# A matmul with a decayed running sum: five of eight scans solved pairwise across ScalarE, GpSimd and VectorE

## The chip, the cores and the metric

The kernel runs on one core of one Trainium2 chip. The metric is the device time of one execution in microseconds, the median of several runs. The kernel before takes 1122.11 us (three runs, 1121.77 to 1122.36).

Each run comes with a state, fast or slow; a run is called slow here when it is over 1.5% above the fastest run of the same kernel.

The engines are named as the profile names them: PE is TensorE, DVE is VectorE, ACT is ScalarE, POOL is GpSimd, SP is SyncE. A trailing q (ACTq, SPq) is the engine's instruction queue, from which it also starts DMA transfers.

## The reference

```
x: (16, 2048, 1024) float32, w: (1024, 1024) float32, decay: (1024,) float32, between 0.05 and 0.95
xw = x @ w
out[:, 0, :] = xw[:, 0, :]
out[:, t, :] = decay * out[:, t - 1, :] + xw[:, t, :]
```

It is a matmul followed by a first-order recurrence along time, separately for each of the 1024 output columns. 134 MB are read and 134 MB are written.

## The kernel before

A "unit" is 1024 time steps of one batch element; there are 32. Each unit has eight "slots" n, one for each block of 128 output columns. TensorE forms the transposed product, with columns on the partitions and time along the free axis, and VectorE's scan instruction runs the recurrence along time (L141, 128x1024, 2252 and 2306 ns). The result is transposed back and stored as 4 MB in four DMAs of 1 MB.

```python
    psp = ctx.enter_context(tc.tile_pool(name="psp", bufs=4, space=bass.MemoryType.PSUM))

    def load(u, l):                       # half a unit: 512 time steps
        xf = xfp.tile([128, 2, NI, CQ], FP32, name="xf")
        for r in range(2):
            for q in range(NQ):
                nc.sync.dma_start(out=xf[q * P:(q + 1) * P, r], in_=...)
        xb = xbp.tile([128, NI, CQ, 2], BF16, name="xb")
        for r in range(2):
            nc.scalar.copy(out=xb[:, :, :, r], in_=xf[:, r])       # the cast, contiguous reads
        xb_of[u, l] = xb
    # turn(u, l): VectorE transposes xb into xt, the operand of the matmul

    for u, (b, h) in enumerate(units):
        for n in range(K):                # 8 slots
            ps = psp.tile([128, TU], FP32, name="ps")
            # ... 16 matmuls into ps ...
            so = sop.tile([128, TU], FP32, name="so")
            nc.vector.tensor_tensor_scan(
                out=so, data0=dec[:, n:n + 1].to_broadcast([128, TU]), data1=ps,
                initial=0.0 if h == 0 else last[n], op0=ALU.mult, op1=ALU.add)
            # ... ScalarE keeps the last column; VectorE transposes the slot before into ot ...
            # ... n == 0: store the unit before; n == 1 and 5: turn and load the next x ...

        def store(u, ot):
            for q in range(NQ):
                nc.scalar.dma_start(out=..., in_=ot[q * P:(q + 1) * P])   # ScalarE's queue
```

The loads are issued from SyncE's queue, the stores from ScalarE's. ScalarE also casts x to bf16, four casts in a unit.

## Time and profile before

| quantity | before | where it is read |
|---|---|---|
| time | 1122.1 us | runs |
| VectorE busy, 400 to 1000 us | 99% | table by stage |
| TensorE busy, same stretch | 91%, granted clock 0.96 | table by stage |
| stores of successive units apart, same stretch | 31.7 us | timeline |
| four stores hold ScalarE's queue, from 312 us on | 9 to 13 us | timeline |

The first part of the page lists busy time, share of the span and number of instructions for each engine:

```profile
PE 932.3 (83%) x4096; PEld 408.4 (36%) x4096; DVE 1013.7 (90%) x584; ACT 324.1 (29%) x257; POOL 0.2 (0%) x4
```

The table by stage shows two stretches from the middle of the run. The columns are the stretch, its length, the busy time and instruction count of each engine, the granted TensorE clock, the share of the DMA engines' time and the GB/s:

```profile
core 0: us, PE busy (x) PEld busy (x) DVE busy (x) ACT busy (x) POOL busy (x), PEclk, DMA share, GB/s
400.00:600.00 200.00, 183.29 (x815) 80.74 (x813) 198.09 (x114) 59.96 (x49) 0.00 (x0) 0.97 1.08 262
...
800.00:1000.00 200.00, 179.59 (x792) 78.78 (x790) 197.74 (x114) 69.02 (x56) 0.00 (x0) 0.95 1.07 267
```

VectorE is busy 198 of every 200 us. TensorE is not far behind with 180 to 183. The groups by line give for each kind of instruction its shapes, its count, then total busy time and the mean in ns of one instruction, and then the engine's idle time just before it with what ended that idle time:

```profile
line engine op names shapes xcount | busy us, mean ns | idle before us <-releasers
L133 PE MATMUL ps<-xt,wsb 128*128 128x512 bf16 x4096 | 932.3, 389 | 157.7 <-DVE xt L106 95.0 <-DVE so L141 42.7 <-DVE wsb L77 19.6
...
L97 ACT CAST xb<-xf 128x2048 bf16<-128x2048 f32 x128 | 310.8, 2474 | 306.2 <-DVE ot L115 100.3 <-DMA xf<-in_x_dram 94.3 <-issue 69.6
L115 DVE STREAM_TRANSPOSE ot<-so 128x1024 f32<-128x1024 f32 x256 | 309.3, 1224 | 3.7
L141 DVE TENSOR_TENSOR_SCAN so<-dec,keep,ps 128x1024 f32<-128x1024 f32 x128 | 295.1, 2306 | 6.4 <-PE ps L133 6.4
L141 DVE TENSOR_TENSOR_SCAN so<-dec,ps 128x1024 f32<-128x1024 f32 x128 | 285.3, 2252 | 20.6 <-PE ps L133 20.6
L106 DVE STREAM_TRANSPOSE xt<-xb 128x2048 f32<-128x2048 f32 x64 | 146.2, 2285 | 44.6 <-ACT xb L97 42.7 <-ACT keep L151 1.8
```

A unit costs VectorE eight scans of 2.28, eight transposes back of 1.22 and two transposes of x of 2.29: together 32.6 us with these means. The scans hardly ever wait for TensorE (6.4 and 20.6 us in all), so VectorE sets the pace.

The busy shares hide something on ScalarE. This is its timeline around one store; the columns are the start, the duration, engine, line, operation and how many instructions are joined:

```profile
start us, us, engine line op out<-in xcount [idle before <-releaser]
498.22 2.48 ACT L97 CAST xb<-xf 128x2048 bf16<-128x2048 f32 x1 [2.10 <-DMA xf<-in_x_dram]
...
503.24 11.40 ACTq L169 DMA_DIRECT2D out_dram<-ot  x4
514.81 4.82 ACT L97 CAST xb<-xf 128x2048 bf16<-128x2048 f32 x2 [14.06 <-DMA out_dram<-ot]
```

The ACTq line is the engine issuing four stores. It takes 11.40 us, and the next cast starts only when it is over. This time is not counted as busy, so ScalarE's 29% says little about how free it is.

The waits of the SyncE queue; the columns are the total, the number of waits and the longest:

```profile
SPq L91 <- DMA out_dram<-ot: 326.5, 36, 30.3
```

Loads wait for stores. In this trace the DMAs issued from SyncE's queue and those from ScalarE's carry the same eight semaphore numbers, 99 to 106. The load that starts at 513.84 waits on number 99, which the store issued at 503.24 carries; the last landing of that store is at 513.82.

### The profile page before, as it was taken

The page shows a single profiled execution, that of the slowest core. Times are in us where ns is not written, and L with a number is a line of the kernel's source. Part 1 is how long each engine was busy: PE and PEld are TensorE (multiplying, and loading weights), DVE is VectorE, ACT ScalarE, POOL GpSimd, SP SyncE. Part 2 cuts the span into 40 slices and gives each one's busy share as a digit, 9 for nine tenths or more (in the row PEclk, how much of TensorE's full clock was granted, in tenths as well). Part 3 has the DMA queues.
Part 4 walks back from the last instruction along what each step waited for, and adds up shares of the span by engine and source line. Part 5 has one row for each costly group of instructions (what it writes and reads, how often), then busy time and mean ns, then how long its engine had stood idle before and what let it go on. Part 6 is the DMA issues. An engine that isn't in the chain of part 4 may idle for free.

```text
span 1123.0 us, 10242 instructions
## 1 busy us (share of the span) xinstructions
PE 932.3 (83%) x4096; PEld 408.4 (36%) x4096; DVE 1013.7 (90%) x584; ACT 324.1 (29%) x257; POOL 0.2 (0%) x4
## 2 busy tenths in 40 slices
PE   0287698796998998989898998989898998989880
PEld 0133243242443443434343443434343443434330
DVE  1295699798999999999999999999999999999991
ACT  2124122242422405151422405151422405151200
POOL 0000000000000000000000000000000000000000
PEclk9997799797999998999999899989999898999995
DMA  9949898999999999999999999999999999999777
GB/s 194 203 81 228 163 268 198 260 275 252 283 272 276 252 276 260 249 273 266 279 264 252 259 279 269 252 274 266 271 264 259 256 277 247 274 278 236 150 145 155
DMA packets 275056, 273.33 MB, mean 243 GB/s; under 512 B 11840, under 2 KB 273984, under 8 KB 275008
## 3 DMA queue, kind: packets, MB, share of 16 engines
q1 hardware_dynamic: 140800, 138.45, 55.5%
q10 hardware_dynamic: 134208, 134.23, 45.5%
q8 instruction: 32, 0.52, 0.2%
q14 instruction: 16, 0.13, 0.0%
HBM read 138.42 MB, written 134.22 MB: 243 GB/s over the span
## 4 chain that ended last, share of the span: by engine, by line
DVE 41%; DMA 27%; issue 9%; SPq 8%; PE 7%; ACTq 3%; ACT 2%; DVEq 0%
DVE so L141 24%; DMA xf<-in_x_dram 15%; DVE ot L115 11%; DMA out_dram<-ot 11%; SPq L91 8%; PE ps L133 7%; DVE xt L106 6%; ACTq L169 3%; ACT xb L97 2%; DMA xf<-in_w_dram 1%; DMA dec<-in_decay_dram 1%; SPq L76 0%; ACT keep L151 0%; ACTq L64 0%; DVE wsb L77 0%
## 5 line engine op out<-in xcount | busy, mean ns | idle before, releaser
L133 PE MATMUL ps<-xt,wsb 128*128 128x512 bf16 x4096 | 932.3, 389 | 157.7 <-DVE xt L106 95.0
L133 PEld LDWEIGHTS <-wsb 128*128 128x128 bf16 x4096 | 408.4, 100 | 681.0 <-issue 204.2
L97 ACT CAST xb<-xf 128x2048 bf16<-128x2048 f32 x128 | 310.8, 2474 | 306.2 <-DVE ot L115 100.3
L115 DVE STREAM_TRANSPOSE ot<-so 128x1024 f32<-128x1024 f32 x256 | 309.3, 1224 | 3.7
L141 DVE TENSOR_TENSOR_SCAN so<-dec,ps 128x1024 f32<-128x1024 f32 x128 | 285.3, 2252 | 20.6 <-PE ps L133 20.6
L141 DVE TENSOR_TENSOR_SCAN so<-dec,keep,ps 128x1024 f32<-128x1024 f32 x128 | 295.1, 2306 | 6.4 <-PE ps L133 6.4
L106 DVE STREAM_TRANSPOSE xt<-xb 128x2048 f32<-128x2048 f32 x64 | 146.2, 2285 | 44.6 <-ACT xb L97 42.7
L151 ACT COPY keep<-so 128x1 f32<-128x1 f32 x128 | 21.1, 186 | 429.7 <-DVE so L141 329.5
L77 DVE CAST wsb<-xf 128x1024 bf16<-128x1024 f32 x8 | 5.4, 687 | 9.8 <-DMA xf<-in_w_dram 9.8
L97 ACT ACT_TABLE_LOAD x1 | 1.3, 1283 | 8.8 <-DMA xf<-in_x_dram 8.8
L190 POOL MEMSET const-uint8-127<- 128x1 uint8 x1 | 0.1, 102 | 0.0
L190 POOL MEMSET const-bfloat16-1.0<- 128x1 bf16 x1 | 0.1, 101 | 0.0
L190 POOL MEMSET const-float32-0.0<- 128x1 f32 x1 | 0.1, 98 | 0.2 <-issue 0.2
L190 POOL MEMSET const-float32-1.0<- 128x1 f32 x1 | 0.1, 98 | 0.0
## 6 DMA issues: line engine op xcount, KB each, us to landing
xf<-in_x_dram SPq DMA_DIRECT2D x512, 256.0 KB, 8.3
out_dram<-ot ACTq DMA_DIRECT2D x128, 1024.0 KB, 13.3
xf<-in_w_dram SPq DMA_DIRECT2D x32, 128.0 KB, 4.0
dec<-in_decay_dram ACTq DMA_DIRECT2D x4, 1.0 KB, 5.6
```

The lines of the kernel that those rows point to most:

```text
L77: nc.vector.tensor_copy(out=wsb[:, k].rearrange("p n q i -> p q n i"), in_=wv.rearrange("p (q n i) -> p q n i", q=NQ, n=K))
L91: nc.sync.dma_start(out=xf[q * P:(q + 1) * P, r], in_=_ap(x, [[2 * D, P], [64 * D, NI], [1, CQ]], (b * S + t0 + r) * D + q * CQ))
L97: nc.scalar.copy(out=xb[:, :, :, r], in_=xf[:, r])
L106: nc.vector.transpose(out=dst.rearrange("p k (i t) -> p i k t", t=P), in_=src.rearrange("p (i k t) -> p i k t", k=K, t=P))
L115: nc.vector.transpose(out=ot[:, :, n * P:(n + 1) * P], in_=so.rearrange("p (i t) -> p i t", t=P))
L133: nc.tensor.matmul(out=ps[:, l * TL:(l + 1) * TL], lhsT=wsb[:, k, n].rearrange("p q i -> p (q i)"), rhs=xt[:, k, l, :], start=(k == 0), st ...
L141: nc.vector.tensor_tensor_scan(out=so, data0=dec[:, n:n + 1].to_broadcast([128, TU]), data1=ps, initial=0.0 if h == 0 else last[n], op0=AL ...
L151: nc.scalar.copy(out=keep, in_=so[:, TU - 1:TU])
L169: nc.scalar.dma_start(out=_ap(out, [[D, P], [P * D, TU // P], [1, CQ]], (b * S + h * TU) * D + q * CQ), in_=ot[q * P:(q + 1) * P])
L190: nc = _bacc.Bacc("TRN2", target_bir_lowering=False, num_devices=1)
```

## The change

VectorE is the bound, so the change takes scan work off it. For the five slots 0, 1, 3, 4 and 6 the recurrence is solved in pairs of time steps:

```
odd:   y[2i+1] = d*d * y[2i-1] + (d * x[2i] + x[2i+1])     a scan of half length
even:  y[2i]   = d * y[2i-1] + x[2i]                       no recurrence
```

ScalarE copies PSUM to SBUF (xs). GpSimd forms d\*x[2i] + x[2i+1] with a multiply and an add. VectorE scans the 512 odd steps. ScalarE scales the shifted odd results by d, and GpSimd adds the even inputs. Slots 2, 5 and 7 keep the full scan. The PSUM tiles for products go from four to three, as d\*d now takes a place in PSUM.

In the same change, w is loaded in whole rows (4 KB for each row, issued from ScalarE's queue, cast by GpSimd). Row p\*8+k goes to partition p, and therefore the cast of x has to gather every eighth column. The first two and the last two groups of work are half units, to shorten the start and the tail; the very last one has no paired slots.

```diff
-    psp = ctx.enter_context(tc.tile_pool(name="psp", bufs=4, space=bass.MemoryType.PSUM))
+    psp = ctx.enter_context(tc.tile_pool(name="psp", bufs=3, space=bass.MemoryType.PSUM))
+    pdp = ctx.enter_context(tc.tile_pool(name="pdp", bufs=1, space=bass.MemoryType.PSUM))
+    PAIRED = (0, 1, 3, 4, 6)
 ...
+        wrows = w.rearrange("(p k) d -> p k d", k=K)
         for k in range(K):
 ...
-            for q in range(NQ):
-                r0 = q * CQ + k * P
-                nc.sync.dma_start(out=wv[q * P:(q + 1) * P, :], in_=w[r0:r0 + P, :])
+            nc.scalar.dma_start(out=wf[:, k], in_=wrows[:, k])
 ...
-        for r in range(2):
-            nc.scalar.copy(out=xb[:, :, :, r], in_=xf[:, r])
+        nc.scalar.copy(
+            out=xb_of[c][:, :, :, :, r],
+            in_=xf_of[c][:, r].rearrange("p i (c k) -> p i k c", k=K))
 ...
+        def pair(self):
+            nc.scalar.copy(out=self.xs, in_=self.ps)
+            ...                                          # first element of so, on GpSimd
+            nc.gpsimd.tensor_scalar(
+                out=h, in0=self.xs[:, 0:T:2], scalar1=dec[:, n:n + 1],
+                scalar2=None, op0=ALU.mult)
+            nc.gpsimd.tensor_tensor(
+                out=self.xs[:, 1:T:2], in0=h, in1=self.xs[:, 1:T:2], op=ALU.add)
+        def scan(self):
+            if self.paired:
+                nc.vector.tensor_tensor_scan(
+                    out=so[:, 3:T + 2:2],
+                    data0=dec2[:, n:n + 1].to_broadcast([128, T // 2]),
+                    data1=self.xs[:, 1:T:2], ...)
+            else: ...                                    # as before, from ps
+        def complete(self):
+            if self.paired:
+                ...
+                nc.scalar.activation(
+                    out=h, in_=so[:, 1:T + 1:2], func=Copy, scale=dec[:, n:n + 1])
+                nc.gpsimd.tensor_tensor(
+                    out=so[:, 2:T + 2:2], in0=h, in1=self.xs[:, 0:T:2], op=ALU.add)
+            ...                                          # keep copies, now on GpSimd
 ...                                                     # stores stay on ScalarE's queue
```

## The prediction

> **What bounds it now.** VectorE. The table by stage (200–1000 us) shows it busy 189, 198, 198 and 198 of each 200 us; TensorE 178–184 at a granted clock of 0.93–0.97. By groups, a unit of 1024 rows costs VectorE eight scans (2.25–2.31 us), eight transposes back (1.22) and two transposes of x (2.29): 32.4 us. The stores start every 31.8 us in the timeline. TensorE's work is about 28.4 us a unit[...]. DMA engines are also occupied throughout (share 1.07, 267 GB/s).
>
> **The hidden resource is ScalarE's queue.** Its busy share is only 29%, but it issues the stores, and an issue holds the engine. Four 1 MB stores occupy it 9.1–13 us in each unit (timeline: 11.4 at 503 us, and the next cast starts only after it); even at the end, with no loads beside them, 9.2. "Not counted as busy" hides 10–12 us of 32.
>
> **What changes per unit.**
> - VectorE: five scans go to half length, an estimated 1.2 us each: 32.4 falls to about 27.
> - GpSimd: per paired tile a half-length multiply and two half-length adds.[...] the trace of before has no such instruction.[...]
> - ScalarE: five PSUM copies[...] and five scaled half-length copies[...].[...] The cast now also reads with a stride of eight elements; it may get slower. Sum: stores 10 + casts 9.9[...] = 28.7 us without one wait.
> - Start: w arrives in 4 KB rows beside x, and six slots run by k; the first unit now starts at 48.6 us; I expect work from about 25 us and 15–20 us saved. Tail: 33 us after the last matmul shrinks to about 12 (half unit, two stores).
>
> **Critical path.** PSUM buffers drop from four to three, and a paired slot frees its buffer only by ScalarE's copy. In ScalarE's order: copy of slot 0, the stores, a cast, then the copy of slot 1. TensorE has three tiles (10.6 us) of lead; stores, cast and copy take 13 or more: about 5 us idle. Then slot 2's scan stands on VectorE behind slot 1's, which waits for copy and GpSimd pair[...]. ScalarE then runs copies, scaled copies and casts in order, waiting on GpSimd and VectorE inside; the last cast of the next x ends near 28 us after the stores began, its transpose near 32, and only then can the next unit's slot 0 run and the next stores be issued: about 36–38 us a unit by hand addition, against 32. Gaining 20–35 us at both ends does not pay for 30 × 4–6 us.
>
> **Prediction:** 1190 us, range 1060 to 1290. Faster by over 2%: 0.23; within 2%: 0.08; slower by over 2%: 0.69.
>
> **Right if:** stores 34 us or more apart; VectorE busy about 70–75%; TensorE idle before ps waiting on ScalarE's copy and on xt; ScalarE's copy of slot 1 directly behind the four store issues; GpSimd below 65%.
> **Wrong if:** store issue holds ScalarE under 6 us; the compiler puts copies ahead of the stores; GpSimd's steps are much shorter. Then TensorE bounds it, near 1000–1050. Worse than predicted if the strided cast or GpSimd's strided steps take twice the estimates.

The forecast was added up with them: ScalarE's sum came to 28.7 us a unit with the terms for the copies that are now cut; the step "13 or more: about 5 us idle", the 28 and 32 us and the 36–38 us a unit contain cut terms as well, and 1190 us rests on them. What can be traced: 178–184 of 200 us at 31.8 us a unit are 28.3 to 29.3 us of TensorE (the text has 28.4), and the 1.2 us of a half-length scan is an estimate of a little over half of the measured 2.25–2.31 (the trace after has 1.22 and 1.28). The 9.1–13 us of store issue are seen from 312 us on; in four of the six units before, the hold was 14.4 to 22.1 us.

## The result, and the profile after

The changed kernel takes 1398.27 us (median of four runs, 1397.18 to 1398.88); the kernel before, in the same rounds, 1122.23. The ratio is 1.2453, with a 95% interval of 1.2432 to 1.2475. Here and below a ratio is the mean time of one kernel's fast runs over that of the other's of the same rounds, so it is not quite the ratio of the quoted medians. The results are correct. The time lies 208 us above the predicted 1190 and outside the range.

The page's first part:

```profile
PE 1021.9 (73%) x4096; PEld 428.7 (31%) x4096; DVE 865.1 (62%) x609; ACT 758.4 (54%) x459; POOL 708.7 (51%) x816
```

The table by stage, with the columns as before:

```profile
400.00:600.00 200.00, 151.84 (x620) 64.48 (x619) 128.74 (x87) 117.29 (x70) 106.26 (x121) 0.90 0.88 201
...
800.00:1000.00 200.00, 153.20 (x615) 64.24 (x613) 129.20 (x86) 115.98 (x67) 103.44 (x116) 0.88 0.87 202
```

VectorE has less to do, as intended: 865.1 us in the whole run instead of 1013.7, and 129 of 200 us in these stretches instead of 198. Nothing took its place as a busy engine: TensorE fell to 152 and 153, ScalarE is at 116 and 117 and GpSimd at 103 and 106. No engine is full (the busiest, TensorE, has 73%) and the time is longer, so the time is in the waits between engines. Busy times and waits by group:

```profile
L135 PE MATMUL ps<-xt,wsb 128*128 128x512 bf16 x4096 | 1021.9, 414 | 362.5 <-ACT xs L167 190.4 <-DVE so L191 121.0 <-DVE xt L122 50.8
L113 ACT CAST xb<-xf 128x2048 bf16<-128x2048 f32 x128 | 505.7, 3952 | 45.7 <-DVE xt L122 26.4 <-DMA xf<-in_x_dram 7.3 <-DVE ot L214 6.8
...
L214 DVE STREAM_TRANSPOSE ot<-so 128x1024 f32<-128x1024 f32 x240 | 293.0, 1231 | 85.1 <-POOL so L207 83.0
L173 POOL TENSOR_SCALAR h<-xs,dec 128x512 f32<-128x512 f32 x150 | 241.3, 1609 | 214.8 <-ACT xs L167 213.4 <-DVE ot L214 1.4
L176 POOL TENSOR_TENSOR xs<-h,xs 128x512 f32<-128x512 f32 x150 | 194.2, 1294 | 11.2
L207 POOL TENSOR_TENSOR so<-h,xs 128x512 f32<-128x512 f32 x150 | 192.7, 1295 | 97.1 <-ACT h L204 97.1
L167 ACT COPY xs<-ps 128x1024 f32<-128x1024 f32 x150 | 148.6, 1011 | 272.2 <-DVE ot L214 78.3 <-DMA xf<-in_x_dram 58.5 <-issue 53.1
L122 DVE STREAM_TRANSPOSE xt<-xb 128x2048 f32<-128x2048 f32 x64 | 145.9, 2279 | 17.9 <-ACT xb L113 17.9
L204 ACT ACTIVATE h<-so,dec 128x512 f32<-128x512 f32 x150 | 113.2, 770 | 233.0 <-DVE so L182 202.1 <-issue 30.9
```

Three things are to be seen here. The cast takes 3952 ns where it took 2474. GpSimd's multiply takes 1609 ns, and its adds 1294 and 1295 (for the 256 elements of the half units 943, and 737 and 738). The instructions that stayed on VectorE did not get slower beside GpSimd: the transposes take 1231 and 2279 ns, before 1224 and 2285.

The longest waits between engines (an answer of the waits view; total, times, longest):

```profile
...
DVE so L182 <- POOL xs L176: 349.2, 139, 12.1
POOL h L173 <- ACT xs L167: 245.3, 82, 21.1
ACT h L204 <- DVE so L182: 219.2, 67, 5.1
PE ps L135 <- ACT xs L167: 190.4, 47, 6.7
PE ps L135 <- DVE so L191: 121.0, 51, 6.2
```

TensorE waits for ScalarE to free a PSUM tile (190.4 us) and for VectorE to do so (121.0). VectorE waits for GpSimd's pairs (349.2), and ScalarE and GpSimd wait for each other's results. A stretch of ScalarE's timeline:

```profile
643.86 1.01 ACT L167 COPY xs<-ps 128x1024 f32<-128x1024 f32 x1
644.52 0.32 ACTq L227 DMA_DIRECT2D out_dram<-ot  x1
644.76 3.99 ACT L113 CAST xb<-xf 128x2048 bf16<-128x2048 f32 x1
644.88 8.57 ACTq L227 DMA_DIRECT2D out_dram<-ot  x3
653.55 1.01 ACT L167 COPY xs<-ps 128x1024 f32<-128x1024 f32 x1 [4.79 <-POOL so L169]
654.46 3.96 ACT L113 CAST xb<-xf 128x2048 bf16<-128x2048 f32 x1
658.32 1.42 ACT L204 ACTIVATE h<-so,dec 128x512 f32<-128x512 f32 x2
659.64 3.92 ACT L113 CAST xb<-xf 128x2048 bf16<-128x2048 f32 x1
663.46 1.92 ACT L167 COPY xs<-ps 128x1024 f32<-128x1024 f32 x2
```

Between 644.52 and 653.45 the queue issues four stores; one cast runs beside that. The copy of slot 1 starts at 653.55, 0.10 us after the issue ends. (The bracket names an instruction of GpSimd as the one that ended the wait; the queue's own issue, which stands before the copy in the same order, is not counted there.) Then a cast is ahead of the two scaled copies, and a further cast is ahead of the next two PSUM copies. The prediction pictured a chain of this kind. The order, however, is not quite the written one: the compiler places an engine's instructions differently from the program text, and it put casts ahead of copies.

In every fourth unit the hold is longer, about 16 us, and not because of issuing:

```profile
518.45 15.40 ACTq L227 DMA_DIRECT2D out_dram<-ot  x3
...
533.95 1.01 ACT L167 COPY xs<-ps 128x1024 f32<-128x1024 f32 x1 [11.59 <-DMA xf<-in_x_dram]
```

Three stores have been issued by 521.6 us. In the trace the fourth starts at 533.53, just after a load that carries the semaphore number it waits on, 103, has landed (533.51). So a store waits about 12 us for a load here, and ScalarE waits with it.

### Where the 274 us of the profiled executions went

The profiled executions lasted 1123.0 and 1396.7 us. The starts of the stores divide them at the same amount of finished work:

| stretch | before | after | difference |
|---|---|---|---|
| start to the store of the second unit | 128.57 | 137.68 | +9.1 |
| the next 29 units | 944.54 (32.57 each) | 1210.29 (41.73 each) | +265.8 |
| from there to the end | 49.9 | 48.7 | −1.2 |

Nearly everything is in the steady units. Between 400 and 1000 us the stores are 31.7 us apart before and 41.55 after. With TensorE's busy share in that stretch (546.79 and 459.35 of 600 us), a unit before is 28.9 us of TensorE work and 2.8 us idle; a unit after is 31.8 us of work and 9.7 us idle. What the idle time after was spent on, in that stretch alone:

```profile
L135 PE MATMUL ps<-xt,wsb 128*128 128x512 bf16 x1836 | 460.1, 416 | 140.7 <-ACT xs L167 84.3 <-DVE so L191 56.3
```

That is 5.8 us a unit behind ScalarE's copies and 3.9 behind VectorE's full scans, and nothing behind the transposed x. The work itself grew by 2.9 us, and the granted clock was 0.88 instead of 0.96 in that stretch (28.9 × 0.96 / 0.88 = 31.5, an estimate from these figures). In some runs the clock was low where TensorE idled much (0.934 at 83% busy, 0.879 at 73%, 0.771 at 56%), but the profiled run of g7_nopairs_plain_pool_written had 0.902 at 83%, so no rule follows, and no run separates this term from the idling.

### The profile page after: what moved, and what is told of

Same layout as the page of the kernel before. It is cut to its first block, busy times and chain, and to the rows that moved or that the text cites. A ratio compares the mean times of both kernels' runs of the same rounds, so it can differ in the third digit from the quotient of the medians.

```text
span 1396.7 us, 11671 instructions
## 1 busy us (share of the span) xinstructions
PE 1021.9 (73%) x4096; PEld 428.7 (31%) x4096; DVE 865.1 (62%) x609; ACT 758.4 (54%) x459; POOL 708.7 (51%) x816
## 4 chain that ended last, share of the span: by engine, by line
DMA 21%; ACT 17%; issue 16%; POOL 15%; ACTq 11%; DVE 11%; SPq 5%; PE 4%; DVEq 0%; POOLq 0%
DMA xf<-in_x_dram 15%; ACT xb L113 11%; ACTq L227 10%; POOL h L173 6%; POOL xs L176 5%; SPq L102 5%; DMA out_dram<-ot 4%; PE ps L135 4%; POOL so L207 3%; ACT xs L167 3%; DVE so L191 3%; DVE ot L214 3%; ACT h L204 3%; DVE so L182 2%; DVE xt L122 2%
## 5 line engine op out<-in xcount | busy, mean ns | idle before, releaser
L135 PE MATMUL ps<-xt,wsb 128*128 128x512 bf16 x4096 | 1021.9, 414 | 362.5 <-ACT xs L167 190.4
L113 ACT CAST xb<-xf 128x2048 bf16<-128x2048 f32 x128 | 505.7, 3952 | 45.7 <-DVE xt L122 26.4
L173 POOL TENSOR_SCALAR h<-xs,dec 128x512 f32<-128x512 f32 (+1 forms) x165 | 255.4, 1548 | 246.7 <-ACT xs L167 245.3
L214 DVE STREAM_TRANSPOSE ot<-so 128x1024 f32<-128x1024 f32 (+1 forms) x272 | 314.9, 1168 | 92.2 <-POOL so L207 89.7
L167 ACT COPY xs<-ps 128x1024 f32<-128x1024 f32 (+1 forms) x165 | 157.1, 972 | 300.1 <-DVE ot L214 78.3
L204 ACT ACTIVATE h<-so,dec 128x512 f32<-128x512 f32 (+1 forms) x165 | 120.9, 748 | 250.1 <-DVE so L182 219.2
L207 POOL TENSOR_TENSOR so<-h,xs 128x512 f32<-128x512 f32 (+1 forms) x165 | 203.7, 1244 | 103.7 <-ACT h L204 103.7
L182 DVE TENSOR_TENSOR_SCAN so<-dec,keep,xs 128x512 f32<-128x512 f32 (+1 forms) x85 | 103.7, 1220 | 219.3 <-POOL xs L176 215.0
L176 POOL TENSOR_TENSOR xs<-h,xs 128x512 f32<-128x512 f32 (+1 forms) x165 | 205.2, 1244 | 12.3
L122 DVE STREAM_TRANSPOSE xt<-xb 128x2048 f32<-128x2048 f32 x64 | 145.9, 2279 | 17.9 <-ACT xb L113 17.9
L191 DVE TENSOR_TENSOR_SCAN so<-dec,keep,ps 128x1024 f32<-128x1024 f32 (+1 forms) x59 | 121.5, 2059 | 13.0 <-PE ps L135 12.9
L191 DVE TENSOR_TENSOR_SCAN so<-dec,ps 128x1024 f32<-128x1024 f32 (+1 forms) x48 | 104.9, 2186 | 24.3 <-PE ps L135 24.3
## 6 DMA issues: line engine op xcount, KB each, us to landing
ot<-in_w_dram ACTq DMA_DIRECT2D x8, 512.0 KB, 10.3
```

What stands on the lines that cost most here:

```text
L113: nc.scalar.copy(out=xb_of[c][:, :, :, :, r], in_=xf_of[c][:, r].rearrange("p i (c k) -> p i k c", k=K))
L122: nc.vector.transpose(out=xt.bitcast(FP32).rearrange("p k (i t) -> p i k t", t=P), in_=src.rearrange("p (i k t) -> p i k t", k=K, t=P))
L135: nc.tensor.matmul(out=ps, lhsT=wsb[:, k, n].rearrange("p q i -> p (q i)"), rhs=xt[:, k, :], start=(k == 0), stop=(k == K - 1),)
L167: nc.scalar.copy(out=self.xs, in_=self.ps)
L173: nc.gpsimd.tensor_scalar(out=h, in0=self.xs[:, 0:T:2], scalar1=dec[:, n:n + 1], scalar2=None, op0=ALU.mult)
L176: nc.gpsimd.tensor_tensor(out=self.xs[:, 1:T:2], in0=h, in1=self.xs[:, 1:T:2], op=ALU.add)
```

## The experiments

The theory after seeing the result: the mechanism of the prediction holds. ScalarE works in order through stores, casts and copies, and three PSUM tiles do not cover its absences. The loss is larger than predicted because the strided cast takes longer and because GpSimd's steps and the order cost more. The first rival: the pairing itself, its handovers between four engines, loses the time, whatever the cast and the stores do. The second rival: the rest of the rewrite (three PSUM tiles, other order, half units) loses it without any pairing.

All kernels gave correct results. All had three timed rounds.

| label | cast | stores from | pairs | order | us | ratio to before |
|---|---|---|---|---|---|---|
| after | strided | ScalarE | yes | compiler's | 1398.3 | 1.245 |
| e2_plain_cast | contiguous | ScalarE | yes | compiler's | 1322.1 | 1.177 |
| g4_stores_pool | strided | GpSimd | yes | compiler's | 1328.1 | 1.183 |
| g1_plain_pool | contiguous | GpSimd | yes | compiler's | 1181.5 | 1.053 |
| e4_no_pairs | strided | ScalarE | no | compiler's | 1279.3 | 1.140 |
| g3_nopairs_plain | contiguous | ScalarE | no | compiler's | 1273.5 | 1.134 |
| e1_stores_sp | strided | SyncE | yes | compiler's | 1758.0 | 1.566 |
| e3_both | contiguous | SyncE | yes | compiler's | 1583.9 | 1.411 |
| s4_split_stores | strided | two each | yes | compiler's | 1975.5 | 1.761 |
| s2_plain_split | contiguous | two each | yes | compiler's | 1909.2 | 1.702 |
| p1_written_order | strided | ScalarE | yes | written | 1531.2 | 1.365 |
| p2_both_written | contiguous | SyncE | yes | written | 1185.2 | 1.055 |
| p3_plain_written | contiguous | ScalarE | yes | written | 1411.4 | 1.258 |
| p4_nopairs_written | strided | ScalarE | no | written | 1446.2 | 1.289 |
| s1_plain_split_written | contiguous | two each | yes | written | 1410.3 | 1.257 |
| g5_plain_pool_written | contiguous | GpSimd | yes | written | 1228.1 | 1.094 |
| g7_nopairs_plain_pool_written | contiguous | GpSimd | no | written | 1135.0 (one fast run) | not given |
| s3_before_split | before, stores two each | | | compiler's | 1790.8 | 1.596 |
| g2_before_pool | before, stores on GpSimd | | | compiler's | 1328.2 | 1.183 |

The expectations were mostly too low. My theory gave a range of times for 17 of these 18 runs (for g3_nopairs_plain only two conditional limits); 16 were missed, all on the slow side, and only the one fast run of g7_nopairs_plain_pool_written fell inside its range.

### First group: cast, store queue, pairing

**e2_plain_cast.** w is loaded in blocks of 32 rows again, so that the cast reads contiguously; all else as after.

```diff
-            nc.scalar.dma_start(out=wf[:, k], in_=wrows[:, k])
+            for q in range(NQ):
+                r0 = q * CQ + k * P
+                nc.scalar.dma_start(out=wf[quad(q), k], in_=w[r0:r0 + P, :])
...
-            in_=xf_of[c][:, r].rearrange("p i (c k) -> p i k c", k=K))
+            in_=xf_of[c][:, r].rearrange("p i (k c) -> p i k c", k=K))
```

> Only edit to the changed kernel: w is loaded in blocks of 32 rows (32 issues and not 8), so that the cast of x reads its input contiguously. Casts should go back from 3.95 us to about 2.47, that is 5.9 us less of ScalarE per unit. Theory Q: nearly all of it shows, since the casts stand in the queue between copies: 36-38 us a unit, 1220-1290 us. Rival G: the casts are beside the path, under 4% change, over 1345 us.

Measured: 1322.11 us, ratio 1.1769 (1.1739 to 1.1799). That lies between the two expectations: the theory had at most 1290 us, the rival over 1345. Two groups of its profile:

```profile
L136 PE MATMUL ps<-xt,wsb 128*128 128x512 bf16 x4015 | 989.3, 406 | 318.7 <-ACT xs L168 158.4 <-DVE so L192 100.3 <-DVE xt L123 55.0
...
L114 ACT CAST xb<-xf 128x2048 bf16<-128x2048 f32 x128 | 317.0, 2481 | 39.0 <-DVE xt L123 27.3 <-DMA xf<-in_x_dram 11.6
```

The cast is back at 2481 ns. The stride alone therefore made it 1471 ns longer, and taking it away is worth 76 us of the 276. No run tried another stride, so why a stride of eight costs this, and from which stride on, was not shown. The order of ScalarE's instructions is nearly that of after (in some units one cast stands before the first store and not behind it), so this comparison is the cleanest. TensorE still idles 318.7 us, 158.4 of it behind ScalarE's copy, so the cast is not all.

**e1_stores_sp.** The stores are issued from SyncE instead of ScalarE, to remove the hold.

```diff
-                nc.scalar.dma_start(       # in store()
+                nc.sync.dma_start(
```

> Only edit to the changed kernel: the output stores are issued from SyncE's queue and not from ScalarE's. Theory Q (ScalarE's in-order queue bounds the changed kernel: each unit of 1024 rows holds it for about 9 us of store issue, 16 us of casts, 5 us of PSUM copies and 4 us of scaled copies, with waits between): the distance between stores falls from about 41.5 us to 33-35, time 1130-1200 us, and TensorE's wait for ScalarE's copy falls from 190 us to under 80. Rival G (the trip of a paired slot through ScalarE, GpSimd, VectorE and GpSimd, with three PSUM buffers, sets the pace, whoever issues stores): under 4% change, over 1345 us.

Measured: 1757.98 us, ratio 1.5658 (1.5615 to 1.5701). It is far slower than after itself, so it shows something else than the hold. The loads now stand behind the stores in SyncE's queue, and the compiler had put the four casts in one block behind the last slot. TensorE idles 751.3 us, 730.1 of it waiting for the transposed x.

**e3_both.** Both edits together.

```diff
+ the edits of e1_stores_sp and e2_plain_cast
```

> Both edits to the changed kernel: stores from SyncE's queue, and contiguous casts. Theory Q: ScalarE has about 19 us of work in a unit, so the bound moves to TensorE (28.4 us at the clock of before) and VectorE (27): 29-32 us a unit, 960-1060 us, which would beat the kernel before. Rival G: over 1300 us.

Measured: 1583.94 us, ratio 1.4106. The same picture as in the run before (559.4 us of TensorE idle on the transposed x). Neither run isolates the hold.

**e4_no_pairs.** The rewrite with every slot on the full scan.

```diff
-    PAIRED = (0, 1, 3, 4, 6)
+    PAIRED = ()
```

> Only edit to the changed kernel: no slot is paired, all eight scans run at full length from PSUM on VectorE; strided casts, stores on ScalarE's queue, three PSUM buffers and the new start and tail stay. ScalarE then has casts (16 us) and stores (9) alone, VectorE 32.4 us a unit again. Both theories: near the kernel before, 1090-1150 us, VectorE busy over 90%. If it stays above 1200 us, then neither pairing theory holds and the loads, the strided cast or the three PSUM buffers by themselves cost it.

Measured: 1279.3 us, ratio 1.1396 (1.1369 to 1.1424). Without pairing the rewrite is 119 us faster than with it. It is nevertheless 14% slower than before. TensorE idles 282.4 us on the transposed x. In the compiled order both transposes of x stand behind the last transpose back of a unit, and the four casts run in a row after the store has been issued. The second rival has a part in the loss: 157 us of the 276 are there with no pair at all. The waits point to the order and the store issue; this run does not separate them from the three PSUM tiles.

### Second group: the written order kept

Because the compiler's order had moved in three of these four kernels, I repeated them with every engine held to the order of the program text.

```diff
+class InOrder:
+    def __init__(self, tc, engine):
+        self.tc, self.engine = tc, engine
+    def __getattr__(self, name):
+        call = getattr(self.engine, name)
+        return lambda *a, **k: self.tc.keep_in_program_order(call(*a, **k))
...
+    scalar_q = InOrder(tc, nc.scalar)      # and the other four engines
...
-            nc.scalar.copy(...)
+            scalar_q.copy(...)             # and so for every instruction
```

**p1_written_order** (after, written order).

> Only edit to the changed kernel: on every engine each instruction is pinned behind the one written before it, so that the compiler cannot move casts, copies or stores against one another (the order that the prediction reckoned with). Theory O (in the first four runs the order that the compiler chose for ScalarE, with the casts of the next x moved to other places, decides as much as the work does): a clear change, over 4% either way; by the prediction's own sum with the measured durations (casts 3.95, GpSimd multiply 1.6, stores 9.2) about 41 us a unit, 1330-1420 us. Rival W (work and waits decide, the order hardly): 1398 within 2%.

Measured: 1531.24 us, ratio 1.3649. Between 400 and 1000 us the stores are 46.2 us apart on average. This tests the method of the prediction, which added durations along the written order. The sum with the measured durations, before the run, gave about 41 us a unit and 1330 to 1420 us, so it missed. (A sum made after the run, with the cast 1.48 longer four times in a unit and the pair step at its measured 2.9, gives 44 to 46 us; it starts from the prediction's sum, and it tests nothing.) The path itself is the one that the prediction describes: TensorE waits 5.5 us a unit for slot 1's copy and 7.4 for the transposed x (186.0 and 256.1 us in the whole run), and in the unit that starts at 603.93 the last cast ends 36.1 us after the first store issue, where the prediction had 28. So for the written order the path was right and the sum too short. The compiler's own order is better than the written one by 133 us.

**p3_plain_written** (the same with the contiguous cast).

> Contiguous casts as in e2_plain_cast (1322 us), stores still on ScalarE's queue, written order pinned. Theory O with the queue theory Q: 35-37 us a unit, 1160-1230 us. Without a role of the order: 1322 within 2%.

Measured: 1411.4 us, ratio 1.2577, 41.8 us a unit. With the order fixed, the stride is worth 120 us, more than the 76 in the compiler's order.

**p2_both_written** (contiguous cast, stores on SyncE).

> Stores from SyncE's queue and contiguous casts as in e3_both (1584 us), and the written order pinned. Theory O: e3 was slow because its four casts stood together behind the last slot; in the written order they are spread, ScalarE has 19 us of work a unit, and the time falls to 1000-1120 us. If SyncE's queue itself is the trouble (loads behind stores that wait for the last transpose), it stays over 1350 us.

Measured: 1185.19 us, ratio 1.0553 (1.0492 to 1.0614), 35.0 us a unit between 400 and 1000 us. It differs from e3_both in the order alone, and it is 399 us faster. TensorE still idles 191.9 us on the transposed x, and one DMA queue now carries loads and stores (268.48 MB, its packets 95.3% of the 16 engines' span). Against p3_plain_written it is 226 us faster: with the written order kept, the store's queue is worth that much.

**p4_nopairs_written** (no pairs, strided cast, stores on ScalarE).

> No slot paired as in e4_no_pairs (1279 us; there all four casts stood behind the store issue and TensorE waited 282 us for x), written order pinned. Theory O: the casts are spread again, VectorE is busy over 92%, 1090-1160 us, near the kernel before. If it stays over 1240 us, the strided cast or the three PSUM buffers cost it whatever the order.

Measured: 1446.17 us, ratio 1.2886. Slower than with the compiler's order by 167 us. Again the version without pairs is faster than its partner with pairs, p1_written_order, here by 85 us. The limit (over 1240 us: the strided cast or the three PSUM tiles cost it whatever the order) was passed. The last run, with the same three tiles and the same order but contiguous casts and stores on GpSimd, takes 1135 us in its one fast run, so the tiles alone are not the reason.

### Third group: stores split between two queues

```diff
-                nc.scalar.dma_start(       # in store()
+                (nc.sync if q % 2 else nc.scalar).dma_start(
```

The idea was to halve the hold on ScalarE, and to do the same to the kernel before as a control.

**s4_split_stores** (after).

> Only edit to the changed kernel: two of the four 1 MB stores of a unit are issued from SyncE's queue, two stay on ScalarE's. In every trace so far the first two issues are accepted in 0.3 and 0.6 us and the next two take 2.4 to 5.7 us each, so the hold on ScalarE should fall from 9.2 to about 1 us, and loads do not all stand behind stores. Theory Q (the hold is a main term): 34-37 us a unit, 1160-1260 us. Rival G (trip through GpSimd with three PSUM buffers): over 1340 us. The compiler's order may shift again; the trace has to show where the casts stand.

**s2_plain_split** (e2_plain_cast).

> Split stores as in s4 and contiguous casts as in e2_plain_cast (1322 us), order by the compiler. Theory Q: both terms gone, 30-33 us a unit, 1000-1100 us. Rival G: over 1260 us.

**s1_plain_split_written** (p3_plain_written).

> As s2, with the written order pinned. p2_both_written had 1185 us with all transfers on one queue, whose packets took 95% of the 16 engines;[...] 30-32 us a unit, 990-1080 us, and a time under the kernel before. If the DMA engines as such bound p2, it stays within 3% of 1185.

**s3_before_split** (the kernel before).

> The kernel before, with the split stores as its only edit. VectorE is its bound (198 of 200 us busy), so freeing ScalarE from 10 us a unit should gain little: 1095-1130 us, within 2% of before. A gain over 3% would mean that the store hold cost the kernel before too, through late casts.

Measured: 1975.48, 1909.19, 1410.29 and 1790.76 us; ratios 1.7608, 1.7021, 1.257 and 1.5962. In s1_plain_split_written the hold did fall to 0.9 us, and the time stayed at that of p3_plain_written, because the cast now waited 311.9 us for loads. The control shows why these runs fail. The waits of SyncE's queue in s3_before_split:

```profile
SPq L91 <- DMA out_dram<-ot: 1050.8, 90, 30.9
```

Before it was 326.5 us in 36 waits. With two stores in the loads' queue the loads wait three times as long for landed stores; how much of it is the order in the queue and how much the common semaphore numbers seen in before, the run does not separate. The kernel before suffers as well (its compiled order changed too), so this group says nothing about the hold in the changed kernel. All four are failed experiments.

### Fourth group: stores on GpSimd's queue

With the stores started from GpSimd the loads keep their queue, and no load waits for a store: the waits of SyncE's queue in g4_stores_pool list none at the line of the loads (after has 317.4 us in 31 waits there). One issue takes 0.78 us of GpSimd's busy time (782 ns in g4_stores_pool, 779 in g1_plain_pool).

```diff
-                nc.scalar.dma_start(       # in store()
+                nc.gpsimd.dma_start(
```

**g4_stores_pool** (after).

> Only edit to the changed kernel: the stores are issued from GpSimd's queue; SyncE's queue keeps the loads alone, ScalarE issues nothing after the start, and the compiled program shows that a load no longer waits for a store's semaphore. Theory Q (the store hold on ScalarE, 9 us of 41.5 a unit, is a main term): 33-36 us a unit, 1130-1230 us, even if GpSimd pays some us for the issue. Rival G (trip through GpSimd with three PSUM buffers): over 1340 us, or slower than 1398 if the issue holds GpSimd instead.

Measured: 1328.1 us, ratio 1.1825 (1.1808 to 1.1843): 70 us less than after. Again this is between the two expectations (at most 1230, over 1340). ScalarE's order is no longer that of after.

**g1_plain_pool** (e2_plain_cast).

> Contiguous casts as in e2_plain_cast (1322 us) and stores from GpSimd's queue. Theory Q: both terms gone, 30-33 us a unit, 1000-1090 us. Rival G: over 1260 us.

Measured: 1181.51 us, ratio 1.0526 (1.0508 to 1.0543): 141 us less than e2_plain_cast, and between the expectations once more (at most 1090, over 1260). The stores are 34.1 us apart on average (26 intervals). No load waits for a store any more. What TensorE waits for most is now VectorE (131.8 us), and ScalarE waits 301.0 us for VectorE's scans and 154.9 for GpSimd's even times.

The cast and the stores interact. Each alone is worth 76 and 70 us, both together 217. They stand in the same in-order queue, and while one of the two remains, TensorE still waits for ScalarE to free PSUM tiles: 158.4 us in e2_plain_cast, 104.8 in g4_stores_pool, but 10.3 with both gone. The issues are not a small matter here. Four issues hold ScalarE 8.9 to 9.3 us in most units of after, while the last of the four stores lands 24 to 25 us after the first is issued. In the traces of before and after the first of four 1 MB stores takes 0.32 us to issue, the second mostly 0.58, the third and fourth mostly 2.4 to 5.9 (106 of 124). The runs without that hold on ScalarE are 70 and 141 us faster, with the new compiled order in it (see g2_before_pool below).

**g3_nopairs_plain** (no pairs, contiguous cast, stores on ScalarE).

> No slot paired and contiguous casts, stores on ScalarE's queue, order by the compiler. Against e2_plain_cast (1322 us) it gives what the pairing costs by itself; against e4_no_pairs (1279 us) what the stride of the cast costs where ScalarE has nothing else. If the pairing is the main cost: under 1180 us. If the rest of the rewrite (three PSUM buffers, two transposes of x late in VectorE's order) costs it, it stays over 1230 us.

Measured: 1273.49 us, ratio 1.1342. Without pairs the cast's length hardly matters (1279.3 with the strided one). Against e2_plain_cast, pairing costs 49 us.

**g2_before_pool** (the kernel before, stores on GpSimd), meant as the control.

> The kernel before with the stores on GpSimd's queue as its only edit (GpSimd is idle there). It is the control for s3_before_split (1791 us): if s3 was slow because loads on SyncE's queue stood behind stores or waited for their semaphores, this one must not be slow: 1090-1130 us, bounded by VectorE at about 32 us a unit. If it is slow as well, moving the stores off ScalarE is bad for another reason and runs e1, e3 and s1 to s4 mean something else.

Measured: 1328.23 us, ratio 1.1829. I had thought that the kernel before would be nearly untouched, and that fell. In the compiled order six casts now stand in one block, the loads wait 516.0 us for casts, and TensorE idles 181 us on the transposed x. Each change of the store's queue that was tried in the compiler's order also changed that order. So the 70 and 141 us above are the queue together with what the compiler made of it; they are not the hold alone. The same goes for e1_stores_sp, e3_both and the split stores in the compiler's order.

### Last group: both known costs removed, written order, with and without pairs

These two kernels differ in one line, the list of paired slots, and keep the same written order. They answer what was still open: what the pairing is worth by itself.

```diff
 g1_plain_pool with the InOrder edit                 -> g5_plain_pool_written
-    PAIRED = (0, 1, 3, 4, 6)
+    PAIRED = ()                                     -> g7_nopairs_plain_pool_written
```

**g5_plain_pool_written**

> After with three things put right at once: the cast reads contiguously (w in blocks of 32 rows), the stores are issued from GpSimd's queue, and the written order is kept on every engine. Pairing stays. My theory (the pairing itself is sound; what cost the time was a longer cast, the store's hold on ScalarE and the compiled order, which the prediction did not cost or costed too low): VectorE's work is 27 us a unit, TensorE's about 29, and with nothing held the stores come 29 to 33 us apart; 980 to 1090 us, TensorE idle under 120 us, VectorE 78 to 88% busy. Rival (the chain of five handovers from PSUM copy to GpSimd to scan and back is itself too long for three PSUM tiles, whatever the cast and the stores do): over 1150 us, about as with the compiler's order (1181.5), TensorE idle over 200 us behind ScalarE's copy, GpSimd's pairs or VectorE's scan.

Measured: 1228.05 us, ratio 1.0941 (1.0915 to 1.0967). My theory expected at most 1090, so it missed; the rival's number held. The three longest waits that matter:

```profile
ACT h L31 <- DVE so L31: 451.9, 131, 5.8
...
DVE so L31 <- POOL xs L31: 279.1, 95, 6.2
PE ps L31 <- DVE xt L31: 222.8, 31, 49.8
```

The last line includes 49.8 us at the start.

The two timelines show how it goes. First GpSimd around a store:

```profile
611.70 1.30 POOL L31 TENSOR_TENSOR xs<-h,xs 128x512 f32<-128x512 f32 x1
...
613.05 3.17 POOL L31 DMA_DIRECT2D out_dram<-ot  x4
...
616.38 1.60 POOL L31 TENSOR_SCALAR h<-xs,dec 128x512 f32<-128x512 f32 x1
618.06 1.29 POOL L31 TENSOR_TENSOR xs<-h,xs 128x512 f32<-128x512 f32 x1
```

The pairs of slot 1 start at 616.38, directly after 3.17 us of store issue. The hold is shorter than on ScalarE, but it has moved to another engine of the same chain. Second, ScalarE late in the same unit:

```profile
629.68 0.76 ACT L31 ACTIVATE h<-so,dec 128x512 f32<-128x512 f32 x1 [5.81 <-DVE so L31]
630.35 2.49 ACT L31 CAST xb<-xf 128x2048 bf16<-128x2048 f32 x1
632.70 0.76 ACT L31 ACTIVATE h<-so,dec 128x512 f32<-128x512 f32 x1
633.36 2.45 ACT L31 CAST xb<-xf 128x2048 bf16<-128x2048 f32 x1
```

The scaled copy waited 5.81 us (the number in brackets) for a scan that waited for GpSimd. The cast of the next x stands behind it, and a second pair of the same kind follows. The last cast ends at 635.81, the transpose of x follows, and TensorE starts again at 639.50 after 5.81 us of idle time. The paired solve makes the casts late through ScalarE's order.

**g7_nopairs_plain_pool_written**

> The same kernel with no slot paired, so that the pair of runs differs in the pairing alone. My theory: with no hold and the written order VectorE bounds it again, as in before: 32.4 us of VectorE a unit, so 1090 to 1140 us, VectorE about 90% busy, and the pairing is then worth 30 to 130 us (the other run is faster). Rival: the rewrite's order (three PSUM tiles, x transposed late) costs by itself, 1200 us or more; then what the pairing costs or gains can't be read as a loss of the order. If this run is the faster of the two, the pairing loses time by its own handovers.

Measured: 1168.63, 1167.94, 1134.95 and 1165.29 us. Three of the four runs count as slow against the fastest (granted clock 0.902 to 0.910 against 0.946), and the profiled run is one of the slow ones, so no ratio is given. The one fast run, 1134.95 us, lies inside what my theory expected, 1.0% above before's 1123.35. Its waits, from a slow run, where only the kind is used:

```profile
PE ps L31 <- DVE xt L31: 164.7, 31, 49.5
```

VectorE is busy 183.5 of 200 us in the middle, and no chain across engines is left except casts and transposes of x. Against this kernel the paired one is 93 us slower, or 61 us if even the slow runs are taken. My theory had expected the opposite sign, a paired kernel faster by 30 to 130 us; that fell. The first rival is right for this part: the pairing loses time by itself. Whether by the number of its handovers or by the length of its steps stays open.

### What the runs together say

Pairing against not pairing, all else equal in the text of the kernel (in the rows with the compiler's order, the compiled orders of the two runs differ too):

| setting | without pairs | with pairs | pairs cost |
|---|---|---|---|
| strided cast, stores on ScalarE, compiler's order | 1279.3 | 1398.3 | 119 |
| strided cast, stores on ScalarE, written order | 1446.2 | 1531.2 | 85 |
| contiguous cast, stores on ScalarE, compiler's order | 1273.5 | 1322.1 | 49 |
| contiguous cast, stores on GpSimd, written order | 1135.0 (one fast run) | 1228.1 | 93 |

The sign is the same in all four. One path from after to before, in the order in which I removed things: stride of the cast 76 us, stores off ScalarE's queue 141 us (with the new compiled order), remainder 58 us. Another path through g4_stores_pool gives 70 and 147 us, and a third one, through e4_no_pairs, 119 us for the pairs and 157 us for the rest of the rewrite. So the parts are not additive and no single share can be claimed for each. No version beats the kernel before; the best with pairs is g1_plain_pool, 5.3% slower.

Not tested: fewer paired slots, a fourth PSUM tile, and GpSimd steps of another length. So it is open how much of the pairing's own loss is GpSimd's duration and how much is the number of handovers.

## Why the prediction was right or wrong

The direction and the hold on ScalarE were right. The path that was added up is not the one that sets the pace in the compiled kernel, and its terms were too small. Step by step:

- **"What bounds it now. VectorE."** The reading holds: its load fell to 26.8 us a unit (386.68 of 600 us, at 41.55 us a unit; predicted about 27). That this would not help was also right, since VectorE then waits.
- **"The hidden resource is ScalarE's queue."** Right. The store issue takes 8.9 to 9.3 us in most units, and the copy of slot 1 starts as it ends. In every fourth unit the hold is about 16 us, some 12 of them a wait for a load's semaphore, which the prediction did not have. Moving the stores to GpSimd's queue saved 70 and 141 us, order included.
- **"the last cast of the next x ends near 28 us … its transpose near 32, and only then can the next unit's slot 0 run … about 36–38 us a unit by hand addition".** This is the step that failed. A unit measured 41.55 us in the middle of the run and 41.73 on average, and the path is another one. In the changed kernel TensorE waits for the transposed x only four times, 50.8 us in all, and never after 190 us. From 400 to 1000 us it waits for ScalarE's copies and VectorE's full scans alone, 5.8 and 3.9 us a unit. The terms of the sum were too small as well: the cast was taken at 2.47 us and took 3.95, which is 5.9 us a unit more in ScalarE's queue (15.8 instead of 9.9). GpSimd's pair step took 2.9 us, 1.61 of it the multiply, and GpSimd's work is 21.9 us a unit (315.67 of 600 us), more than the estimates had. PSUM copies took 1.01 us and scaled copies 0.77, close to the estimates. ScalarE's queue thus carries about 9 + 15.8 + 5.1 + 3.9 = 33.8 us where the prediction had 28.7. The prediction itself had warned of the cast ("it may get slower") and left it at the old length in the sum.
- **"about 5 us idle" before slot 1, and a wait behind slot 2's scan.** TensorE's wait for ScalarE's copy is 190.4 us in all, 5.9 a unit; its wait for VectorE's full scan is 121.0, 3.8 a unit. The first had the right size, but in part by luck: between 400 and 1000 us it is mostly (15 of 18 waits) not the copy of slot 1 that ends the wait but the next one, behind two casts and two scaled copies (at 663.46 in the timeline above). The second came true as a wait; its predicted size was below the measured one. TensorE's work was 2.9 us a unit longer at the lower clock (0.88 instead of 0.96), which the prediction did not have.
- **"15–20 us saved" at the start.** Wrong: the second unit's store starts 9.1 us later than before. The first matmul came at 31.6 us (19.6 before, where the first ones stand singly). No run separates the causes of this.
- **"Tail: 33 us after the last matmul shrinks to about 12."** Right as it stands (12.3 us from the last matmul at 1384.4 to the end). But it gained only 1.2 us, since the last two half units take longer to get there.
- **The number itself.** The middle of the prediction's own terms is 1122 + 30 × 5 − 27.5 = 1244. I put 1190, to leave weight on the case that the hold would not bite. That alone is 54 us of the 208. The rest is 29 units at 9.16 instead of 5 us (121 us) and both ends (about 8 us lost instead of 27.5 gained, 35 us).
- **The written order.** I assumed it. The compiler's order was another, and 133 us faster than the written one (p1_written_order), where the path of the prediction is found but takes 46.2 us a unit. So the error in the sum and the error about the order partly cancelled, which was luck.
- **The "right if" list.** Stores over 34 us apart, the copy of slot 1 directly behind the issues and GpSimd below 65% (51%) came true. VectorE at 70 to 75% did not: it is at 62%, because the time got longer. TensorE waiting on ScalarE's copy came true, waiting on xt did not. The case named as worse than predicted, twice the estimates, was not needed: the cast grew 1.6-fold, from 2.47 to 3.95 us. "Wrong if … the compiler puts copies ahead of the stores" did not happen for slot 1.

## What to carry to other kernels

Taking work off the busiest engine can cost more than it saves if the replacement passes through several in-order engines for each tile: here the busy time of VectorE fell by 15% and the time rose by 25%, and the pairing itself lost 49 to 119 us in all four comparisons. Of the 276 us, 157 stood even without any pair; what the three PSUM tiles did to the paired chain was not tested. Before adding work to an engine that looks idle, add up its queue with DMA issues included (here 29% busy, and 9 to 13 of 32 us a unit held by issues beside that), and give every instruction whose access pattern changes a new duration and not the old one (here 3.95 instead of 2.47 us). The edits that moved the stores to another queue also changed the compiled order and what the loads wait for (516.0 us for casts in g2_before_pool, 1050.8 for stores in s3_before_split), so make a control on the kernel before and a pair with the order held, and read the order from the trace before crediting the edit.
